# Seven gate panels ahead of the RWKV chunk solve, four between its small products, five left for later

## The chip, the cores and the metric

The kernel runs on one core of a Trainium2 chip. The metric is the device time in microseconds of one execution: 2214.5 us before the change, the median of three runs (2211.7 to 2218.17). One further execution was recorded by the hardware profiler; all rows below come from it.

## The reference

A block with four attention mixers and a feed-forward layer is followed by a second block, and only that one is touched. Its 512 tokens of width 1024 are projected once, and the projection is split into an RWKV-7 branch, a sparse-attention branch (DSA) and 2048 gate columns:

```
z = rmsnorm(h, norm_mix) @ w_in
z_rw, z_dsa, z_gate = _split(z, (RW_COLS, DSA_COLS, GATE_COLS))
y_a = rwkv7_branch(z_rw, ...)
y_b = dsa_branch(z_dsa, kv_norm, w_uk, w_uv)
g_a, g_b = jnp.split(jax.nn.sigmoid(z_gate + b_gate), 2, axis=-1)
h = h + (g_a * (y_a @ w_proj_a) + g_b * (y_b @ w_proj_b)) @ w_out
h = h + cross_attention(...); h = h + hier_moe(...)
# rwkv7_branch: a state of 64 x 64 for each of 8 heads, token by token
    sa = jnp.einsum('bhij,bhj->bhi', state, -kk_t)
    state = state * w_t + sa[..., None] * (kk_t * a_t) + v_t[..., None] * k_t
    y_t = jnp.einsum('bhij,bhj->bhi', state, r_t)
# dsa_branch: an indexer scores all keys for every query and keeps the best
    iscore = jnp.einsum('bqh,bqhs->bqs', w_idx, relu(q_idx . k_idx));  _, idx = lax.top_k(iscore, k_sel)
    softmax attention of 8 heads over the selected latent keys
```

The gates z_gate depend on nothing but the normed input, so they can be computed at any time before the two branches are merged.

## The kernel before

A gate panel is 128 of the 2048 gate columns. Its product is summed over eight blocks of 128 inputs, and each float32 weight and input is split into a high and a low fp32r part, so one panel is 24 matmuls of 128x512 (high by high, high by low, low by high; `mm3`, line 135). `panel` loads the raw weights in two halves by DMA on SyncE's (SP's) queue, casts the high part on ScalarE (ACT, line 125) and subtracts to get the low part on GpSimd (POOL, line 128). `fills` computes panels as fillers: they write PSUM buffers "f" of their own and use a pool of weight buffers that doesn't stand in the way of the work beside them. The result goes through a tanh on ACT and to DRAM (`gtd`).

The RWKV recurrence is computed in chunks of 64 tokens, 8 chunks for 4 pairs of heads:
- `rwkv_prep` makes the chunks' matrices (`Mt`) and values (`VA`).
- `rwkv_solve` solves the triangular system of each chunk. `from_values` (line 1365) makes products of 64x64 into `LV`, copied out of two PSUM buffers "s" by ACT and VectorE (DVE) in turn. The inverse of 128 triangular blocks of 32x32 is done on DVE alone (lines 1387 and 1389, 62 dependent operations); its input NT and its results Z go through DRAM. Then TensorE (PE) puts the halves together: 64 products of 32x32 (line 1409), 64 more (line 1417), and 128 products of 64x64 (lines 1423 and 1426).
- `rwkv_scan` carries the state over the eight chunks, `rwkv_out` normalizes by head (group norm) and applies the RWKV output gate.

`dsa_index` (lines 1533 to 1580) projects the indexer's queries and keys (into PSUM "tp"), scores (lines 1559 and 1560) and takes the best keys of three query blocks by 16 rounds each of MAX8 (line 1571) and MATCH_REPLACE (line 1572) on DVE. `dsa` attends; its first softmax operation is line 245. Behind it come the other gates as fillers and `mem_kv`, the keys and values of the memory for the cross attention.

What sets the order: a list scheduler gives each engine a fixed queue of instructions. It goes through the program in the order in which it is written and takes what its model of the readiness allows, earlier lines first, so a line that is written early is preferred and one that is written late fills gaps. `tc.issue_after` fixes an order between instructions beyond that. On the chip each engine takes its queue strictly in order. Before, the gates 0 to G2_AHEAD - 1 = 7 are written behind `dsa_index`, and the gates 8 to 15 behind `dsa`.

Of the kernel before, what the change touches and what calls it, by code (L numbers as in the profile page):

```python
# [20 lines left out]
G_BUFS = 18  # L21
G2_BUFS = 7
BD_BUFS = 2
G2_AHEAD = 8
DI_BUFS = 6
DG_BUFS = 10
DB_BUFS = 8
# [18 lines left out]
class Core:  # L46
# [90 lines left out]
    def fills(self, items, hi, lo, n=T, how=True):  # L137

        self.filling = how
        for src, done in items:  # L140
            done(self.fm(src, hi, lo, n))
        self.filling = False

    def acc(self, name="acc"):
        if name not in self.pb:
# [1205 lines left out]
        nc.sync.dma_start(kbd[:, :, p].rearrange("c p t -> p c t"), KB)  # L1351


def rwkv_solve(K, pool, Mt, VA, Wm):

    nc, tc, a = K.nc, K.tc, K.a
    nd = tc.dram_tile([P, 1024], F32, name="ndd")
    zd = tc.dram_tile([P, 2, 1024], F32, name="zdd")

    def from_values(i):  # L1360
        t = pool.tile([P, 2, 512], F32, name="LV", bufs=3)
        for s in range(2):
            pl = K.acc("s")
            for c in range(8):
                nc.tensor.matmul(pl[64:128, c * 64:(c + 1) * 64], Mt[0:64, i, s, c, 0:64],
                                 VA[0:64, i, c, 64 * s:64 * s + 64], start=True, stop=True, tile_position=(0, 64))
            K.copy(t[64:128, s], pl[64:128])
        return t

    LV = [from_values(i) for i in range(3)]  # L1370

    with nc.allow_non_contiguous_dma(reason="blocks"):
        for i in range(4):
            for b in range(2):
                nc.sync.dma_start(bass.AP(tensor=nd.tensor, offset=nd.offset + (i * 32 + b) * 1024,
                                          ap=[[32, 32], [2048, 16], [1, 32]]),
                                  Mt[64 + 32 * b:96 + 32 * b, i].rearrange("p s c t -> p (s c) t")[:, :, 32 * b:32 * b + 32])
    NT = pool.tile([P, 32, 32], F32, name="NT")
    nc.sync.dma_start(NT.rearrange("p a b -> p (a b)"), nd)
    Z = pool.tile([P, 32, 32], F32, name="Z")  # L1380
    nc.sync.dma_start(Z.rearrange("p a b -> p (a b)"),
                      bass.AP(tensor=a["eye32"].tensor, offset=a["eye32"].offset, ap=[[0, P], [1, 1024]]))
    for s in range(31):
        w = pool.tile([P, 256], F32, name="ztmp", bufs=1)
        n = 31 - s
        wv = w[:, :(s + 1) * n].rearrange("p (j t) -> p j t", t=n)
        nc.vector.tensor_mul(wv, Z[:, :s + 1, s:s + 1].to_broadcast([P, s + 1, n]),
                             NT[:, s:s + 1, s + 1:].to_broadcast([P, s + 1, n]))
        nc.vector.tensor_add(Z[:, :s + 1, s + 1:], Z[:, :s + 1, s + 1:], wv)
    nc.sync.dma_start(zd[:, 0], Z.rearrange("p a b -> p (a b)"))  # L1390
    nc.vector.tensor_copy(NT, Z.rearrange("p a b -> p b a"))
    nc.sync.dma_start(zd[:, 1], NT.rearrange("p a b -> p (a b)"))
    T1 = Wm.rearrange("p i c t -> p (i c t)").rearrange("p (i s c t) -> p i s c t", i=4, s=2, c=8)
    with nc.allow_non_contiguous_dma(reason="blocks"):

        nc.sync.dma_start(T1[64:96].rearrange("p i s c t -> p (i s c) t"),
                          bass.AP(tensor=zd.tensor, offset=zd.offset + 1024, ap=[[32, 32], [4096, 64], [1, 32]]))
        for b in range(2):
            nc.sync.dma_start(Mt[64 + 32 * b:96 + 32 * b].rearrange("p i s c t -> p (i s c) t")[:, :, 32 * b:32 * b + 32],
                              bass.AP(tensor=zd.tensor, offset=zd.offset + b * 2048,  # L1400
                                      ap=[[32, 32], [4096, 64], [1, 32]]))
    tags = ("acc", "pv", "s", "s")
    Q = Wm.rearrange("p i c t -> p i (c t)")
    for i in range(4):
        pq = K.acc(tags[i])
        for s in range(2):
            for c in range(8):
                o = (s * 8 + c) * 32
                nc.tensor.matmul(pq[96:128, o:o + 32], Mt[64:96, i, s, c, 32:64], T1[64:96, i, s, c], start=True,
                                 stop=True, tile_position=(64, 96))  # L1410
        K.copy(Q[96:128, i], pq[96:128])
    for i in range(4):
        pz = K.acc(tags[i])
        for s in range(2):
            for c in range(8):
                o = (s * 8 + c) * 32
                nc.tensor.matmul(pz[64:96, o:o + 32], Q[96:128, i, o:o + 32], Mt[96:128, i, s, c, 32:64], start=True,
                                 stop=True, tile_position=(96, 64))
        K.copy(Mt[64:96, i, :, :, 32:64], pz[64:96].rearrange("p (s c t) -> p s c t", s=2, c=8))
    for i in range(4):  # L1420

        pw, pu = K.acc(tags[i % 2]), [K.acc("s") for _ in range(2)]
        one = lambda s, c: nc.tensor.matmul(pw[64 * s:64 * s + 64, c * 64:(c + 1) * 64],
                                            VA[64:128, i, c, 64 * s:64 * s + 64], Mt[64:128, i, s, c, 0:64], start=True,
                                            stop=True, tile_position=(64, 64 * s))
        two = lambda s, c: nc.tensor.matmul(pu[s][64:128, c * 64:(c + 1) * 64], Mt[64:128, i, s, c, 0:64],
                                            LV[i][64:128, s, c * 64:(c + 1) * 64], start=True, stop=True,
                                            tile_position=(64, 64))
        for c in range(8):
            two(0, c)  # L1430
            one(0, c)
            two(1, c)
            one(1, c)
        K.copy(Wm[:, i].rearrange("p c t -> p (c t)"), pw)
        for s in range(2):
            K.copy(VA[64:128, i, :, 64 * s:64 * s + 64], pu[s][64:128].rearrange("p (c t) -> p c t", c=8))
        if i == 0:
            LV.append(from_values(3))
# [462 lines left out]
class Experts:  # L1901
# [305 lines left out]
def block2(K, h3, xd, out):  # L2207
# [20 lines left out]
    rwkv_prep(K, K.pool(S, "prep"), hhi, hlo, Mt, VA, eC, xg, kbd, red, bvd)  # L2228
    S.close()
    K.dve_split = ()  # L2230
    DS = ExitStack()
    dp = K.pool(DS, "dsa", "left")
    V = ExitStack()
    vp = K.pool(V, "solve")
    Wm = vp.tile([P, 4, 8, 64], F32, name="Wm")
    I_ = ExitStack()
    rwkv_solve(K, K.pool(I_, "inv"), Mt, VA, Wm)
    I_.close()
    rwkv_scan(K, K.pool(V, "scan"), Mt, VA, Wm, eC, kbd, red, ytd)
    V.close()  # L2240
# [4 lines left out]
    def gate(f):
        def done(z):
            t = rp.tile([P, 512], F32, name="gt", bufs=2)
            nc.scalar.activation(t, z, AF.Tanh, scale=0.5, bias=K.pd["bg"][:, f:f + 1])
            nc.sync.dma_start(gtd[f], t)
        return done  # L2250

    idx = dsa_index(K, dp, hhi, hlo)
    for f in range(G2_AHEAD):
        K.fills([(a["w2f"][22 + f], gate(f))], hhi, hlo, how=f%4==0 or 'main')
    DA = ExitStack()
    datt = K.pool(DA, "datt")
    mk = K.pool(DA, "memkv")
# [212 lines left out]
```

## Time and profile before

| | |
|---|---|
| median of 3 runs | 2214.5 us (2211.7 to 2218.17) |
| the profiled execution: its time, its span | 2219.63 us, 2217.7 us |
| mean granted clock of TensorE | 0.966 |
| busy: PE, DVE, ACT, POOL | 2061.6, 1082.7, 712.7, 486.9 us |
| the second block's stretch from rwkv_prep to the first softmax of dsa | about 1104 to 1342 us |

All times of rows are microseconds from the span's start. PE is the queue of matmuls; the granted clock is the share of full speed (2.4 GHz) that the chip allowed it, 1.00 or 0.50 at a time, a mean over a window. "Busy" on PE includes matmuls that run at half clock. A float32 product of 32x32 or 64x64 has two records, so x32 is 16 products.

### The profile page before, as it was taken

The numbers are of one execution on the slowest core, as the hardware profiler recorded it, in microseconds if no ns is written. First come the engines' busy times: TensorE is split into PE (matmuls) and PEld (weight loads), VectorE is DVE, ScalarE is ACT, GpSimd is POOL, SyncE is SP. The second block draws the span as 40 slices with busy tenths as digits, with TensorE's granted clock in tenths as the row PEclk, the third lists the DMA queues.
The fourth block names the chain that finished last, engine by engine and source line by source line (L and its number), as shares of the span: only waits on it lengthen the run. The fifth ranks groups of instructions, "written<-read, shape, count | busy, mean of one in ns | idle before, by whom it ended". The sixth has DMA issues, their size and how long they took to land. (4 is left out here: it accounts for less than half of the span.)

```text
span 2217.7 us, 28574 instructions
## 1 busy us (share of the span) xinstructions
PE 2061.6 (93%) x10308; PEld 1484.6 (67%) x10308; DVE 1082.7 (49%) x2569; ACT 712.7 (32%) x1510; POOL 486.9 (22%) x389
## 2 busy tenths in 40 slices
PE   6999899999999999978989999999998899998997
PEld 5767676686888888866777867777887344433333
DVE  5272326337763545465787646556444333332223
ACT  4353234423453434334432235543440111000012
POOL 2402232233233222233332121232121000000000
PEclk9999999999999999999998899999998899999999
DMA  5513332257232333133434342475256899999996
GB/s 175 174 44 84 75 104 80 72 175 233 84 118 95 95 97 102 52 113 112 119 109 101 105 163 89 145 252 188 70 188 217 335 419 420 420 420 420 419 421 248
DMA packets 175577, 407.50 MB, mean 184 GB/s; under 512 B 46922, under 2 KB 65482, under 8 KB 150728
## 3 DMA queue, kind: packets, MB, share of 16 engines
q1 hardware_dynamic: 173128, 400.07, 50.8%
q0 software_dynamic: 2304, 5.57, 0.7%
q8 instruction: 83, 1.36, 0.3%
q14 instruction: 62, 0.51, 0.1%
HBM read 370.94 MB, written 33.13 MB: 182 GB/s over the span
## 5 line engine op out<-in xcount | busy, mean ns | idle before, releaser
L128 POOL TENSOR_TENSOR w<-wraw,w 128x512 fp32r<-128x512 f32 x310 | 409.3, 1331 | 1068.1 <-ACT w L125 966.2
L125 ACT CAST w<-wraw 128x512 fp32r<-128x512 f32 (+1 forms) x446 | 261.8, 616 | 238.0 <-issue 51.9
L135 PE MATMUL f<-hhi,w 128*128 128x512 f32 (+1 forms) x832 | 279.7, 408 | 1.6 <-POOL w L128 0.6
L135 PE MATMUL f<-h2hi,w 128*128 128x512 f32 (+1 forms) x672 | 203.9, 384 | 0.4 <-POOL w L128 0.4
L128 DVE TENSOR_TENSOR w<-wraw,w 128x512 fp32r<-128x512 f32 (+1 forms) x136 | 112.5, 829 | 165.0 <-ACT w L125 160.7
L135 PEld LDWEIGHTS f<-hhi,w 128*128 128x128 f32 x832 | 160.5, 198 | 34.8 <-issue 3.2
L135 PE MATMUL acc<-hhi,w 128*128 128x512 f32 (+1 forms) x512 | 168.6, 396 | 11.1 <-DVE ks L1233 7.4
L135 PE MATMUL f<-hlo,w 128*128 128x512 f32 (+1 forms) x416 | 169.1, 407 | 0.2 <-DVE hlo L187 0.2
L135 PEld LDWEIGHTS f<-h2hi,w 128*128 128x128 f32 x672 | 125.3, 188 | 25.4 <-POOL w L128 0.6
L135 PE MATMUL f<-h2lo,w 128*128 128x512 f32 (+1 forms) x336 | 129.1, 384 | 0.0
L2096 PE MATMUL s<-mw,hT 128*64 128x512 f32 x416 | 107.0, 596 | 14.6 <-DMA mw<-wexp 14.6
L135 PEld LDWEIGHTS acc<-hhi,w 128*128 128x128 f32 x512 | 95.9, 190 | 35.0 <-DVE ks L1233 7.6
L2049 PE MATMUL f<-mw,xT 128*64 128x512 f32 x416 | 108.6, 597 | 10.8 <-DMA mw<-wexp 10.6
L135 PE MATMUL acc<-hlo,w 128*128 128x512 f32 (+1 forms) x256 | 100.7, 393 | 0.0
L135 PEld LDWEIGHTS f<-hlo,w 128*128 128x128 f32 x416 | 82.2, 198 | 16.0 <-issue 1.4
L2004 POOL DMA_INDIRECT xs<-xnd,row x13 | 12.9, 991 | 336.9 <-DVE tg L2009 282.6
L2096 PEld LDWEIGHTS s<-mw,hT 128*64 128x64 f32 x416 | 35.8, 137 | 74.5 <-issue 47.6
L2049 PEld LDWEIGHTS f<-mw,xT 128*64 128x64 f32 x416 | 33.2, 137 | 75.3 <-issue 50.2
L2100 DVE SCALAR_TENSOR_TENSOR ylo<-s,tg,yhi 128x512 fp32r<-128x512 f32 x32 | 24.0, 751 | 114.9 <-ACT yhi L2099 114.9
L2099 ACT ACTIVATE yhi<-s,tg 128x512 fp32r<-128x512 f32 x32 | 22.0, 687 | 168.9 <-PE s L2096 162.7
L135 PEld LDWEIGHTS f<-h2lo,w 128*128 128x128 f32 x336 | 63.2, 188 | 12.5
L135 PE MATMUL f<-w,mw 128*128 128x512 f32 x240 | 63.9, 413 | 2.1 <-ACT w L125 1.5
(762 smaller groups left out, 4070.5 us busy)
## 6 DMA issues: line engine op xcount, KB each, us to landing
mw<-wexp SPq DMA_DIRECT2D x155, 1024.0 KB
w<-wexp SPq DMA_DIRECT2D x36, 1024.0 KB
wraw<-wup SPq DMA_DIRECT2D x88, 256.0 KB
wraw<-w2f SPq DMA_DIRECT2D x76, 256.0 KB
wraw<-wgate SPq DMA_DIRECT2D x64, 256.0 KB
wraw<-wdown SPq DMA_DIRECT2D x44, 256.0 KB
wraw<-w1f SPq DMA_DIRECT2D x40, 256.0 KB
gated<-gt SPq DMA_DIRECT2D x28, 256.0 KB
```

The source lines that it names most:

```text
L125: nc.scalar.copy(hi[:, s], raw)
L128: eng.tensor_sub(lo[:, s], raw, hi[:, s].bitcast(F32))
L135: self.nc.tensor.matmul(out, l, r, start=start and i == 0, stop=stop and i == 2)
L2004: nc.gpsimd.indirect_dma_start(xs, None, self.xnd, bass.IndirectOffsetOnAxis(ap=row[:, 0:1], axis=0), bounds_check=T - 1, oob_is_err=False)
L2049: K.last = nc.tensor.matmul(GU[n][w][64 * s:64 * s + 64], xTs[n][:, kk, 64 * s:64 * s + 64], ws[s][k], start=kk == 0, stop=kk == 7)
L2096: K.last = nc.tensor.matmul(o[64 * s:64 * s + 64], hT[:, c, 64 * s:64 * s + 64], ws[s][c], start=c == 0, stop=c == 3)
L2099: nc.scalar.activation(yhi[:, hs], o, AF.Copy, scale=tgs[n][:, 1:2])
L2100: nc.vector.scalar_tensor_tensor(ylo[:, hs], o, tgs[n][:, 1:2], yhi[:, hs].bitcast(F32), op0=OP.mult, op1=OP.subtract)
```

## The change

The gates 0 to 6 (G2_PREP) are now written as fillers ahead of `rwkv_solve`. The gates 7 to 10 (up to G2_AHEAD, now 11) come from a generator, `steps`, three matmuls at a time (eight steps for a gate; the next panel's load is written one gate ahead). `rwkv_solve` calls it through `between`, which puts the small products and the steps into a fixed order: a step behind each sixteen products in the two 32x32 stages, and one or two in turn behind each eight products in the 64x64 stage, 32 steps in all. Five gates instead of eight stay behind `dsa`.

```
@@ -140 @@
+    def steps(self, items, hi, lo):
+        pans = []
+        for n, (src, done) in enumerate(items):
+            self.filling = True
+            pans += [self.panel(s, 1024) for s, _ in items[len(pans):n + 2]]
+            o = self.acc("f")
+            self.filling = False
+            for k in range(8):
+                s = slice(k * P, (k + 1) * P)
+                w = [t[:, s] for t in pans[n]]
+                for i, (a, b) in enumerate(((0, hi), (0, lo), (1, hi))):
+                    self.last = self.nc.tensor.matmul(o, w[a], b[:, k, :], start=k == 0 and i == 0, stop=k == 7 and i == 2)
+                if k == 7:
+                    done(o)
+                yield
@@ rwkv_solve @@
+    def between(products, n):
+        for i in range(0, len(products), n):
+            with tc.issue_after(K.last.ins) if K.last else nullcontext():
+                for p in products[i:i + n]:
+                    K.last = p()
+            with tc.issue_after(K.last.ins):
+                for _ in range(1 + count[0] % 2 if n == 8 else 1):
+                    next(fill, None)
+            count[0] += 1
...
-        for s in range(2):
-            for c in range(8):
-                o = (s * 8 + c) * 32
-                nc.tensor.matmul(pq[96:128, o:o + 32], Mt[64:96, i, s, c, 32:64], T1[64:96, i, s, c], start=True, ...
+        between([lambda s=s, c=c, o=o: nc.tensor.matmul(pq[96:128, o], ...) for s, c, o in at], 16)
...
-        for c in range(8):
-            two(0, c)
-            one(0, c)
-            two(1, c)
-            one(1, c)
+        between([lambda f=f, s=s, c=c: f(s, c) for c in range(8) for f, s in ((two, 0), (one, 0), (two, 1), (one, 1))], 8)
@@ block2 @@
-    rwkv_solve(K, K.pool(I_, "inv"), Mt, VA, Wm)
+    for f in range(G2_PREP):
+        K.fills([(a["w2f"][22 + f], gate(f))], hhi, hlo, how=f % 4 == 0 or "main")
+    fill = K.steps([(a["w2f"][22 + f], gate(f)) for f in range(G2_PREP, G2_AHEAD)], hhi, hlo)
+    rwkv_solve(K, K.pool(I_, "inv"), Mt, VA, Wm, fill)
...
     idx = dsa_index(K, dp, hhi, hlo)
-    for f in range(G2_AHEAD):
-        K.fills([(a["w2f"][22 + f], gate(f))], hhi, hlo, how=f%4==0 or 'main')
```

The line numbers of the changed program are higher: line 135 is 136 and 157 (in `steps`), 178 is 196, 1365 is 1396, 1387 and 1389 are 1418 and 1420, 1409 is 1438, 1423 and 1426 are 1451 and 1454, 1571 and 1572 are 1595 and 1596.

PE where the solve begins, before: the 32x32 products stand in one block between fillers (`f<-`, gate panels).

```order
L135 MATMUL f<-hhi,w 128x512 x2
L135 MATMUL f<-hlo,w 128x512
L135 MATMUL f<-hhi,w 128x512 x2
L135 MATMUL f<-hlo,w 128x512
L1409 MATMUL acc<-Wm,Mt 32x32 x16
L1409 MATMUL pv<-Wm,Mt 32x32 x16
L1409 MATMUL s<-Wm,Mt 32x32 x32
L135 MATMUL f<-hhi,w 128x512 x2
L135 MATMUL f<-hlo,w 128x512
L135 MATMUL f<-hhi,w 128x512 x2
L135 MATMUL f<-hlo,w 128x512
```

And after, from the same place, where index projections (`tp<-`) come first:

```order
L136 MATMUL tp<-hhi,w 128x512 x2
L136 MATMUL tp<-hlo,w 128x512
L1438 MATMUL acc<-Wm,Mt 32x32 x16
L157 MATMUL f<-hhi,w 128x512
L157 MATMUL f<-hlo,w 128x512
L157 MATMUL f<-hhi,w 128x512
L1438 MATMUL pv<-Wm,Mt 32x32 x16
L157 MATMUL f<-hhi,w 128x512
L157 MATMUL f<-hlo,w 128x512
L157 MATMUL f<-hhi,w 128x512
L1438 MATMUL s<-Wm,Mt 32x32 x16
L157 MATMUL f<-hhi,w 128x512
```

Each group of sixteen products has three gate matmuls behind it. In the 64x64 stage, before, 128 products stood without a wide matmul among them for most of the stage; after:

```order
L1454 MATMUL s<-LV,Mt 64x64 x2
L1451 MATMUL acc<-Mt,VA 64x64
L157 MATMUL f<-hhi,w 128x512
L157 MATMUL f<-hlo,w 128x512
L157 MATMUL f<-hhi,w 128x512
L1454 MATMUL s<-LV,Mt 64x64
L1451 MATMUL acc<-Mt,VA 64x64
L1454 MATMUL s<-LV,Mt 64x64
L1451 MATMUL acc<-Mt,VA 64x64
L1454 MATMUL s<-LV,Mt 64x64
L1451 MATMUL acc<-Mt,VA 64x64
```

Here a group is eight products. Ahead of the solve, PE after the change, at the end of 160 fillers in a row and the first values of `from_values`:

```order
L136 MATMUL f<-hhi,w 128x512 x2
L136 MATMUL f<-hlo,w 128x512
L136 MATMUL f<-hhi,w 128x512
L1396 MATMUL s<-VA,Mt 64x64 x16
L136 MATMUL tp<-hhi,w 128x512
L136 MATMUL tp<-hlo,w 128x512
L136 MATMUL tp<-hhi,w 128x512 x2
L1396 MATMUL s<-VA,Mt 64x64 x16
```

The second group (the second row of line 1396) writes the PSUM buffers that the copies of LV read. These copies on DVE, before, with the inversion's first operations behind them:

```order
L178 COPY KB<-tp 128x512
L178 COPY VA<-tp 128x512
L178 COPY LV<-s 64x512 x3
L1534 TENSOR_SCALAR widx<-tp 128x16
L1387 TENSOR_TENSOR ztmp<-Z,NT 128x31
L1389 TENSOR_TENSOR Z<-Z,ztmp 128x31
```

And after, with the inversion's last operations:

```order
L1418 TENSOR_TENSOR ztmp<-Z,NT 128x31
L1420 TENSOR_TENSOR Z<-Z,ztmp 128x31
L1422 COPY NT<-Z 128x1024
L196 COPY LV<-s 64x512 x3
L1558 TENSOR_SCALAR widx<-tp 128x16
L1573 TENSOR_TENSOR dg<-tp,qv 64x384 x2
L196 COPY Wm<-pv 32x512
```

The three copies went from ahead of the inversion to behind it. On DVE in `rwkv_out`, before, no round of the top-k is left:

```order
L187 TENSOR_TENSOR g<-YT,g 128x512
L1504 SCALAR_TENSOR_TENSOR YT<-acc,YT 128x512
L187 TENSOR_TENSOR g<-YT,g 128x512
L1504 SCALAR_TENSOR_TENSOR YT<-acc,YT 128x512
L227 TENSOR_TENSOR ss<-ss 128x1
L187 TENSOR_TENSOR g<-YT,g 128x512
L1504 SCALAR_TENSOR_TENSOR YT<-acc,YT 128x512
L187 TENSOR_TENSOR g<-YT,g 128x512
```

And after, at the same operations (lines 205 and 1528 are 187 and 1504 before):

```order
L205 TENSOR_TENSOR g<-YT,g 128x512
L1595 MAX m_10521<-mask_10450 128x8
L1528 SCALAR_TENSOR_TENSOR YT<-acc,YT 128x512
L1596 MATCH_REPLACE mask_10450<-m_10521,mask_10450 128x512
L1595 MAX m_10551<-mask_10525 128x8
L1597 TENSOR_SCALAR mask_10450<-mask_10450 128x512
L205 TENSOR_TENSOR g<-YT,g 128x512
L1596 MATCH_REPLACE mask_10525<-m_10551,mask_10525 128x384
L1528 SCALAR_TENSOR_TENSOR YT<-acc,YT 128x512
L1595 MAX m_10554<-mask_10525 128x8
```

A round (MAX, MATCH_REPLACE) stands ahead of nearly every operation. Of the 48 rounds, 8 stand in the scan now and 40 between it and the first operation of line 245; before, all 48 stood ahead of the operations shown.

## Rows read from the trace of the kernel before

**Rows 1.** The page: busy time, share and instructions of each engine.
```profile
PE 2061.6 (93%) x10308; PEld 1484.6 (67%) x10308; DVE 1082.7 (49%) x2569; ACT 712.7 (32%) x1510; POOL 486.9 (22%) x389
```

**Rows 2.** Windows over four stages around the solve; columns in the first row.
```profile
core 0: us, PE busy (x) PEld busy (x) DVE busy (x) ACT busy (x) POOL busy (x), PEclk, DMA share, GB/s
1106.00:1190.70 84.70, 73.96 (x363) 58.41 (x361) 72.73 (x156) 24.98 (x54) 27.20 (x20) 0.96 0.43 118
1190.70:1235.00 44.30, 44.30 (x579) 40.92 (x579) 18.29 (x40) 11.16 (x19) 6.21 (x7) 0.62 0.27 81
1235.00:1276.40 41.40, 39.35 (x268) 34.11 (x267) 31.30 (x85) 7.47 (x18) 4.83 (x4) 0.96 0.37 112
1276.40:1342.00 65.60, 61.01 (x250) 43.42 (x249) 31.84 (x86) 23.43 (x46) 16.93 (x13) 0.92 0.44 151
```

**Rows 3.** Windows inside the solve, the same columns.
```profile
1200.00:1205.00 5.00, 5.00 (x61) 3.99 (x61) 1.64 (x4) 0.29 (x1) 0.00 (x0) 0.89 0.69 204
...
1215.00:1235.00 20.00, 20.00 (x194) 18.73 (x193) 5.97 (x13) 6.13 (x11) 6.03 (x7) 0.50 0.23 73
```

**Rows 4.** Timeline of PE (start, us, line): a streak of fillers, ends.
```profile
1147.64 0.40 PE L135 MATMUL f<-hlo,w 128*128 128x512 f32 x1
...
1165.71 0.39 PE L135 MATMUL f<-hhi,w 128*128 128x512 f32 x1
```

**Rows 5.** Timeline of PE behind an idle.
```profile
1169.97 0.38 PE L1559 MATMUL tp<-dg,qv 128*128 128x256 f32 x1 [3.87 <-ACT big L1563]
...
1170.67 0.63 PE L135 MATMUL f<-hlo,w 128*128 128x512 f32 x1
...
1173.23 0.63 PE L135 MATMUL f<-hlo,w 128*128 128x512 f32 x1
```

**Rows 6.** Timeline of PE in the solve.
```profile
1190.74 1.19 PE L1409 MATMUL acc<-Wm,Mt 32*32 32x32 f32 x32
1191.77 1.17 PE L1409 MATMUL pv<-Wm,Mt 32*32 32x32 f32 x32
...
1207.64 0.58 PE L1423 MATMUL acc<-Mt,VA 64*64 64x64 f32 x9
...
1209.64 1.70 PE L1426 MATMUL s<-LV,Mt 64*64 64x64 f32 x14
...
1229.39 3.67 PE L1426 MATMUL s<-LV,Mt 64*64 64x64 f32 x32
...
1234.02 1.91 PE L1480 MATMUL pv<-Mt,VA 128*128 128x128 f32 x8
```

**Rows 7.** Timeline of DVE: the inversion, its first and last rows.
```profile
1119.35 1.06 DVE L1387 TENSOR_TENSOR ztmp<-Z,NT 128x31 f32<-128x31 f32 x1
...
1124.10 0.28 DVE L1389 TENSOR_TENSOR Z<-Z,ztmp 128x112 f32<-128x112 f32 x1
...
1125.79 0.34 DVE L1387 TENSOR_TENSOR ztmp<-Z,NT 128x175 f32<-128x175 f32 x1
1126.17 1.31 DVE L1389 TENSOR_TENSOR Z<-Z,ztmp 128x175 f32<-128x175 f32 x1
...
1170.09 1.08 DVE L1391 COPY NT<-Z 128x1024 f32<-128x1024 f32 x1
```

**Rows 8.** Timeline of POOL beside it.
```profile
1125.81 2.82 POOL L128 TENSOR_TENSOR w<-wraw,w 128x512 fp32r<-128x512 f32 x2 [2.96 <-ACT w L125]
```

**Rows 9.** Timeline of SP's queue: the load for the inversion.
```profile
1110.79 0.33 SPq L1379 DMA_DIRECT2D NT<-ndd  x1
```

**Rows 10.** Windows of lines 1571 and 1572 alone (DVE busy, count).
```profile
1100.00:1360.00 260.00, 26.51 (x48) 0.89 0.39 117
...
1100.00:1360.00 260.00, 29.52 (x96) 0.89 0.39 117
```

**Rows 11.** Timeline of DVE: the first softmax.
```profile
1341.94 0.29 DVE L245 CUSTOM_DVE_ANT_0 big<-s,dmask 128x128 f32<-128x128 f32 x1 [0.48 <-PE s L135]
```

More of the change, by code (lines that the diff above doesn't have):

```diff
@@ L23 @@
 BD_BUFS = 2
-G2_AHEAD = 8
+G2_PREP = 7
+G2_AHEAD = 11
 DI_BUFS = 6
@@ L1351, in rwkv_prep, with rwkv_solve @@
         nc.sync.dma_start(kbd[:, :, p].rearrange("c p t -> p c t"), KB)
-def rwkv_solve(K, pool, Mt, VA, Wm):
+def rwkv_solve(K, pool, Mt, VA, Wm, fill):
     nc, tc, a = K.nc, K.tc, K.a
+    count, K.last = [0], None
+    def between(products, n):
[7 more added lines that the diff above has]
+            count[0] += 1
     nd = tc.dram_tile([P, 1024], F32, name="ndd")
@@ L1403, in rwkv_solve @@
     Q = Wm.rearrange("p i c t -> p i (c t)")
+    at = [(s, c, slice((s * 8 + c) * 32, (s * 8 + c) * 32 + 32)) for s in range(2) for c in range(8)]
     for i in range(4):
         pq = K.acc(tags[i])
-        for s in range(2):
-            for c in range(8):
-                o = (s * 8 + c) * 32
-                nc.tensor.matmul(pq[96:128, o:o + 32], Mt[64:96, i, s, c, 32:64], T1[64:96, i, s, c], start=True,
-                                 stop=True, tile_position=(64, 96))
+        between([lambda s=s, c=c, o=o: nc.tensor.matmul(pq[96:128, o], Mt[64:96, i, s, c, 32:64], T1[64:96, i, s, c],
+                                                        start=True, stop=True, tile_position=(64, 96))
+                 for s, c, o in at], 16)
         K.copy(Q[96:128, i], pq[96:128])
@@ L1413, in rwkv_solve @@
         pz = K.acc(tags[i])
-        for s in range(2):
-            for c in range(8):
-                o = (s * 8 + c) * 32
-                nc.tensor.matmul(pz[64:96, o:o + 32], Q[96:128, i, o:o + 32], Mt[96:128, i, s, c, 32:64], start=True,
-                                 stop=True, tile_position=(96, 64))
+        between([lambda s=s, c=c, o=o: nc.tensor.matmul(pz[64:96, o], Q[96:128, i, o], Mt[96:128, i, s, c, 32:64],
+                                                        start=True, stop=True, tile_position=(96, 64))
+                 for s, c, o in at], 16)
         K.copy(Mt[64:96, i, :, :, 32:64], pz[64:96].rearrange("p (s c t) -> p s c t", s=2, c=8))
@@ L1428, in rwkv_solve @@
                                             tile_position=(64, 64))
-        for c in range(8):
-            two(0, c)
-            one(0, c)
-            two(1, c)
-            one(1, c)
+        between([lambda f=f, s=s, c=c: f(s, c) for c in range(8) for f, s in ((two, 0), (one, 0), (two, 1), (one, 1))], 8)
         K.copy(Wm[:, i].rearrange("p c t -> p (c t)"), pw)
@@ L2230, in block2, with gate, done @@
     K.dve_split = ()
+    def gate(f):
+        def done(z):
+            t = rp.tile([P, 512], F32, name="gt", bufs=2)
+            nc.scalar.activation(t, z, AF.Tanh, scale=0.5, bias=K.pd["bg"][:, f:f + 1])
+            nc.sync.dma_start(gtd[f], t)
+        return done
     DS = ExitStack()
@@ L2236, in block2 @@
     I_ = ExitStack()
-    rwkv_solve(K, K.pool(I_, "inv"), Mt, VA, Wm)
+    for f in range(G2_PREP):
+        K.fills([(a["w2f"][22 + f], gate(f))], hhi, hlo, how=f % 4 == 0 or "main")
+    fill = K.steps([(a["w2f"][22 + f], gate(f)) for f in range(G2_PREP, G2_AHEAD)], hhi, hlo)
+    rwkv_solve(K, K.pool(I_, "inv"), Mt, VA, Wm, fill)
+    for _ in fill:
+        pass
     I_.close()
@@ L2244, in block2 @@
     U.close()
[L2245 to L2250, printed above, removed]
     idx = dsa_index(K, dp, hhi, hlo)
-    for f in range(G2_AHEAD):
-        K.fills([(a["w2f"][22 + f], gate(f))], hhi, hlo, how=f%4==0 or 'main')
     DA = ExitStack()
```

## The prediction

> **What bounds the kernel now.** The page's busy times come first: TensorE is busy 2061.6 us of the span of 2217.7, 93% [rows 1], so only two things can win time, idle of PE and the clock at which it runs. The windows over the four stages between the end of rwkv_prep and the first softmax of dsa say where these lie [rows 2]. In 1106 to 1190.7, the stage before the solve, PE is idle 10.7 us (84.70 less 73.96) at a granted clock of 0.96. In the solve, 1190.7 to 1235, it is never idle (44.30 of 44.30), but the clock is 0.62: of its two levels, 2.4 and 1.2 GHz, it had the lower for most of the stage, and 0.38 x 44.3 = 16.8 us of full-speed work went. The scan to 1276.4 loses 2.1 us by idle, the stretch to 1342 another 4.6. So the solve's clock is the one large loss, and the windows inside it show what goes with it: 1215 to 1235, where PE is busy 20.00 of 20.00 almost only with the 64x64 products, was granted 0.50 throughout, and 1200 to 1205, mostly wide matmuls, had 0.89 [rows 3].
>
> The Trainium skill says in TensorE: Matmul & The Clock Gate, "Why this matters for your kernels", that drops inside a kernel are avoided by having no idle gaps between bursts. This trace doesn't agree for small products: no idle, and 0.50 [rows 3]. By that rule the interleaved matmuls would bring nothing here, since no gap is closed in the solve; it stands with rival 3.
>
> **The prices.** Wide matmul (128x512): 80 of them start between 1147.64 and 1165.71, 18.07/79 = 0.229 us each at full clock, and in all this streak PE never stood, so the panels' loads, casts and subtractions keep up with it [rows 4]. After an idle of 3.87 six of them took 1173.23 - 1170.67 = 2.56, 0.427 each: the half level [rows 5]. Sixteen 32x32 products (32 records) take 1.03 us, from start to start of two groups. Sixteen 64x64 products (32 records) take 2.00 us at full clock (1207.64 to 1209.64, 32 records) and 3.67 at half [rows 6].
>
> **Part one, seven gates ahead of the solve.** Gates 0 to 6 were fillers already; now they stand in front of the chunks' values. 160 of their 168 matmuls come as one streak from 1104.4: 160 x 0.229 = 36.6, to 1141.0. The first sixteen products of from_values (2.0) and four index matmuls (0.9) follow, to 1143.9. The next sixteen wait for a PSUM buffer that a VectorE copy of LV frees, and these copies now stand behind the whole inversion on DVE. Before, they stood ahead of it.
>
> So the inversion's end sets PE's restart. It has 62 dependent operations. Before, it ran from 1119.35, shared DVE with the index work, and ended before the copy of NT at 1170.09 [rows 7]. Alone, the row at 1124.10 gives 0.28 us for n = 112, and from this and its like I take 23.4 us for all 62 with the gaps. Beside a GpSimd subtraction (1125.81, two in 2.82 [rows 8]) an operation took 1.31, where its neighbour of the same size took 0.34 [rows 7]: 0.95 more, and two subtractions come per panel, every 24 x 0.229 = 5.5 us. Solving for the stretch, 23.4 + 1.9 x (length/5.5) gives 36; with a few that meet idle gaps I take 34 (bounds 23.4 and 36). Its start: NT's load was issued at 1110.79 [rows 9]; on SP's queue one more gate store now stands ahead of it, so I put it at 1112.8. The bounds are that moment and the old start of 1119.35; I take 1116.5. Then 34 + the copy of NT 1.1 + the copy of LV 0.7: PE may go on at 1152.3, a wait of 8.4 us (bounds 0 and 14).
>
> After it come 16 + 16 products (4.0), 4 + 16 + 35 index matmuls (12.6) and four transposes (0.5): 17.1. PE restarts at half clock; the six matmuls of rows 5 lost 6 x 0.198 = 1.2 us, and since small products come first here and this wait is twice as long, I take 3.5 (bounds 1.2 and the whole 17.1). The solve begins at 1173 (before: 1190.74). The inverse comes back in time: before, the first product stood 20.6 us behind the copy of NT and had other work ahead of it, and 1150.5 + 20.6 = 1171.
>
> **Part two, four gates between the solve's products.** 96 wide matmuls stand there now, against 29 fillers in a block before. At full clock: eight groups of sixteen 32x32 products and three wide matmuls, 8 x (1.03 + 0.8) = 14.6, where 0.8 is 3 x 0.229 and 0.1 for the change of shape; ten index matmuls 2.3; sixteen groups of eight 64x64 products, 16 x 1.0; behind them eight times three and eight times six wide matmuls, 8 x 0.8 + 8 x 1.47 = 18.2; from_values(3) 2.0. Sum 53.1, and one wait for a PSUM copy of 1 us: 54 us, to 1227 (before 1234, with 67 wide matmuls fewer, or 15.3 us of work). All of this rests on the clock staying up, bounded by "all at half": 96 x 0.198 + 288 x 0.052 = +34. I take full, because the window with wide matmuls among small ones was granted 0.89 [rows 3].
>
> **Part three, what makes room.** The index scores and the top-k move. PE had scored beside the inversion; now it does so in the scan, in the place of gate matmuls, and I leave the scan at its 42.4 us (1234.0 [rows 6] to 1276.4): it ends at 1269.4, 7 us earlier. But the top-k is 48 rounds on DVE, 26.51 + 29.52 = 56.0 us [rows 10], and was hidden beside the inversion, the solve and the scan. Now eight rounds run in the scan, and 40 between the scan's end and the first softmax: up to 40/48 x 56.0 = 46.7 us. DVE had 31.84 us of work in these 65.6 [rows 2]; 78.5 in all is more than the stretch. The rounds depend on each other, and rwkv_out's group norm now has a round ahead of each of its short operations; some 0.16 us between operations in 40 rounds make it 85 (bounds: 65.6, if all hides, and 97). The first softmax, 1341.94 before [rows 11], comes at 1269.4 + 85 = 1354.4, 12.5 us later.
>
> By then PE has done 42 wide matmuls more than it had before at this point (by the order of the instructions: 29 of gates, 13 of the latent queries), 42 x 0.229 = 9.6 us that need not be done later, and dsa and mem_kv behind it are bound by PE. Three gates fewer are left as fillers behind dsa; I cost that at nothing, because mem_kv's matmuls remain to fill its waits, and at up to 72 x 0.229 = 16.5 us if they don't. In the tail PE is idle some 21 us now (85 less the 61.01 of [rows 2] and 2.5 for eleven of the 42, which fall here), against 4.6, and the clock falls more often: 2 us. Sum: 12.5 - 9.6 + 2 = +4.9. The profiled execution took 2219.63 (its span and 1.9 around it), 5.1 above the median of 2214.5; the difference goes on the median: **2219.5**. What can be told from no change is about 0.3%, 6.6 us, so this is inside, on the slow side.
>
> **The rivals.** 1. The top-k hides. If the tail's DVE is not what ends last (PE has latent queries and gate fillers for it, and DVE's extra work needs an arrival only at each block's mask), the stretch keeps 65.6: 1269.4 + 65.6 - 1341.9 = -6.9, less 9.6, and 2 for the clock: -14.5, 2200. For it: DVE was 49% busy there. Against it: 78.5 us don't go into 65.6.
> 2. No wait at the LV copies: the inversion takes 23.4 and ends at 1141.7 with its copies, before PE comes. That saves 8.4 and a part of the restart: 2210. Against it are the GpSimd subtractions, seven panels' worth beside it.
> 3. The clock stays at half in the solve in spite of the wide matmuls; the streak before it then wins nothing and the 96 matmuls pay double: +34, 2253, slower. It decides from the moment PE's granted clock in the solve is under about 0.8. For it: six wide matmuls in a row were not enough at 1170.67 to raise it [rows 5], and here three or six stand together. Against it: the 0.89 of 1200 to 1205 [rows 3].
> 4. Nothing moves. These matmuls were fillers and are so now; what the solve wins the later stages lack, idle for idle: 2214.5.
> 5. The tail is worse than 85: each short operation of the group norm waits for a whole round, ScalarE and PE wait with it, and it takes 97: 2232.
>
> **How the numbers follow.** Forecast 0.42 (its own range 2211 to 2230: 0.01 faster, 0.19 the same, 0.22 slower); rival 1 0.22, all faster; rival 2 0.10 (0.03 faster, 0.07 the same); rival 3 0.08 and rival 5 0.08, slower; rival 4 0.10 (0.01, 0.08, 0.01). Faster 0.27, the same 0.34, slower 0.39. The range of 2200 to 2240 leaves out half of rival 1 and rival 3, 0.19.
>
> **What would show it.** Right: PE idle of some 8 us released by the DVE copy of LV, about 38 us behind rwkv_prep; granted clock above 0.9 in the solve; DVE nearly full from the scan's end to the first softmax, and that stretch some 20 us longer. Wrong: no idle before the second group of from_values (rival 2), a solve over 70 us (rival 3), a stretch from the scan to the first softmax of under 70 us (rival 1).

## The result

The changed kernel took 2239.89 us (median of four runs, 2236.11 to 2252.9), the kernel before 2213.68 us on the same chip (2211.7 to 2218.17). The ratio is 1.0122, 95% interval 1.0092 to 1.0153: slower by 26 us, clear of noise. The forecast was 2219.5 us and no measurable change, leaning to slower; the side was missed, and the time lies at the upper end of the range of 2200 to 2240.

The windows of the changed kernel over the same four stages, cut where they begin now (columns as in [rows 2]):

```profile
1106.00:1179.53 73.53, 65.54 (x338) 53.66 (x338) 38.76 (x75) 17.08 (x30) 21.24 (x17) 0.88 0.48 128
1179.53:1236.29 56.76, 56.76 (x651) 43.17 (x651) 7.61 (x11) 13.92 (x24) 13.46 (x12) 0.94 0.28 90
1236.29:1278.54 42.25, 40.60 (x286) 34.64 (x285) 35.80 (x77) 14.27 (x33) 5.08 (x4) 1.00 0.37 108
1278.54:1373.03 94.49, 72.90 (x273) 51.58 (x272) 74.99 (x213) 28.98 (x61) 19.39 (x15) 0.82 0.37 124
```

Against [rows 2]: the solve's clock rose from 0.62 to 0.94, which is what the change put the gates there for. The scan is as long as before (42.25 us). The stretch from the scan's end to the first softmax grew from 65.6 to 94.5 us. PE is idle there for 21.6 us (94.49 less 72.90; 4.6 before), and its clock is 0.82 (0.92 before). VectorE (DVE) is busy 75.0 us instead of 31.8.

PE's timeline at the places that the forecast names (it answers to [rows 5, 6]; line 252 is 234 before, the transposes of mem_norm):

```profile
1155.87 3.67 PE L1396 MATMUL s<-VA,Mt 64*64 64x64 f32 x32 [7.32 <-DVE LV L196]
...
1179.53 1.19 PE L1438 MATMUL acc<-Wm,Mt 32*32 32x32 f32 x32
1181.54 1.19 PE L1438 MATMUL pv<-Wm,Mt 32*32 32x32 f32 x32
...
1324.29 0.40 PE L136 MATMUL f<-hhi,w 128*128 128x512 f32 x1
1326.34 0.60 PE L1218 MATMUL acc<-ident,gn 128*16 128x128 f32 x4 [1.65 <-DVE gn L1215]
...
1366.46 1.94 PE L252 MATMUL tp<-ident,njunk 128*128 128x128 f32 x8 [9.44 <-DVE njunk L249]
```

The first row is the wait at the copies of LV, 7.32 us. The rows of 1179.53 and 1181.54 are two groups of sixteen products with three gate matmuls between them, 2.01 us. The row of 1324.29 is the last gate matmul ahead of the first softmax: behind it no gate is left to fill in, and PE idles step by step, in the last row 9.44 us for a DVE operation of mem_norm (line 249). Of the 21.6 us of idle 16.7 lie behind this matmul: from 1324.69 to 1373.03 PE is busy 31.68 of 48.34 us, at a clock of 0.75. On DVE that operation stands behind the rounds, and so does the first softmax (it answers to [rows 11]):

```profile
1360.54 0.41 DVE L1596 MATCH_REPLACE8 mask<-m,mask 128x256 f32<-128x256 f32 x1
1360.98 0.43 DVE L1595 MAX8 m<-mask 128x8 f32<-128x256 f32 x1
...
1365.57 1.41 DVE L249 SCALAR_TENSOR_TENSOR njunk<-njunk,ny,g_mem 128x512 f32<-128x512 f32 x2
...
1373.03 0.29 DVE L263 CUSTOM_DVE_ANT_0 big<-s,dmask 128x128 f32<-128x128 f32 x1 [0.44 <-PE s L136]
```

On DVE, ahead of the solve (answers to [rows 7]):

```profile
1120.95 0.97 DVE L1418 TENSOR_TENSOR ztmp<-Z,NT 128x31 f32<-128x31 f32 x1 [10.46 <-DMA NT<-ndd]
...
1126.33 1.31 DVE L1418 TENSOR_TENSOR ztmp<-Z,NT 128x175 f32<-128x175 f32 x1
1127.68 0.34 DVE L1420 TENSOR_TENSOR Z<-Z,ztmp 128x175 f32<-128x175 f32 x1
...
1154.06 1.03 DVE L1422 COPY NT<-Z 128x1024 f32<-128x1024 f32 x1
1155.12 0.69 DVE L196 COPY LV<-s 64x512 f32<-64x512 f32 x1
```

The inversion began at 1120.95 and lasted up to the copy of NT at 1154.06: 33.1 us, with 1.31 against 0.34 us for two operations of one size, one of them beside a GpSimd subtraction.

### The profile page after: what moved, and what is told of

The parts are those of the page before. It is cut to its first block, busy times and chain, and to the rows that moved or that the text cites. A ratio compares the mean times of both kernels' runs of the same rounds, so it can differ in the third digit from the quotient of the medians.

```text
span 2239.0 us, 28568 instructions
## 1 busy us (share of the span) xinstructions
PE 2069.9 (92%) x10308; PEld 1480.2 (66%) x10308; DVE 1075.0 (48%) x2569; ACT 714.1 (32%) x1510; POOL 483.3 (22%) x389
## 5 line engine op out<-in xcount | busy, mean ns | idle before, releaser
L136 PE MATMUL f<-hhi,w 128*128 128x512 f32 (+1 forms) x768 | 249.7, 398 | 1.9 <-ACT w L126 0.6
L136 PE MATMUL acc<-hhi,w 128*128 128x512 f32 (+1 forms) x512 | 173.3, 407 | 13.3 <-DVE ks L1251 7.5
L136 PEld LDWEIGHTS f<-hhi,w 128*128 128x128 f32 x768 | 144.3, 193 | 31.4 <-issue 2.5
L136 PE MATMUL f<-hlo,w 128*128 128x512 f32 (+1 forms) x384 | 152.4, 397 | 0.2 <-DVE hlo L205 0.2
L2073 PE MATMUL f<-mw,xT 128*64 128x512 f32 x416 | 108.6, 597 | 10.7 <-DMA mw<-wexp 10.5
L136 PEld LDWEIGHTS f<-hlo,w 128*128 128x128 f32 x384 | 74.1, 193 | 14.4 <-issue 1.0
L136 PEld LDWEIGHTS f<-h2lo,w 128*128 128x128 f32 x336 | 63.1, 188 | 12.3
```

Source lines behind the costliest of these rows:

```text
L136: self.nc.tensor.matmul(out, l, r, start=start and i == 0, stop=stop and i == 2)
L2073: K.last = nc.tensor.matmul(GU[n][w][64 * s:64 * s + 64], xTs[n][:, kk, 64 * s:64 * s + 64], ws[s][k], start=kk == 0, stop=kk == 7)
```

## The experiments

Theory A was that the top-k rounds displaced to DVE behind the scan are the loss by themselves; B, the wait at LV and the cold clock behind it; C, in this form after the first four runs, that the gates taken into the solve are missing as fillers behind the scan, where the rounds leave PE waiting; E, that interleaving costs by itself. Two of the first expectations use the letter C otherwise: for part one alone it is E, and for one round in the changed kernel it is the missing fillers without the rounds. Times are medians, each with its ratio to the kernel before on the same chip (median there 2209.4 to 2213.7 us). Single executions of one kernel differ by about 1%, so verdicts are drawn from ratios and the profile is read only for where time lies.

**Part one alone.** Built from the kernel before:

```
+    for f in range(7):
+        K.fills([(a["w2f"][22 + f], gate(f))], hhi, hlo, how=f % 4 == 0 or "main")
     rwkv_solve(K, K.pool(I_, "inv"), Mt, VA, Wm)
...
-    for f in range(G2_AHEAD):
+    for f in range(7, G2_AHEAD):
```

> The kernel before with the first part of the change alone: gates 0 to 6 written ahead of the solve, gate 7 behind dsa_index and gates 8 to 15 behind dsa as before; no gate matmul is put between the solve's products. By the order, 26 of the 48 top-k rounds now stand behind the scan (0 before, 33 in the changed kernel, counted from the first operation on YT). Theory A (the displaced top-k rounds on VectorE make the stretch from the scan's end to the first softmax long): the stretch takes about 80 us, the clock in the solve stays near 0.6, and the time is 2225 to 2240. Rival B (the wait for the LV copies behind the inversion and the cold clock after it is the main loss, the rest is neutral): 2213.7 + 7.3 + 4 = 2225, with a stretch of 66 us. Rival C (the interleaving is what costs, by the changes of shape in the solve): 2214.

Measured: 2212.79 us, ratio 0.9999 (0.9968 to 1.0031): no change. A and B missed the time, and the third theory (C there, E here) gave it with 2214. The stretch is near A's 80 us all the same; windows of the solve and of the stretch behind the scan:

```profile
1179.90:1215.84 35.94, 35.94 (x562) 34.19 (x561) 8.72 (x13) 9.17 (x17) 4.74 (x5) 0.67 0.21 66
...
1261.71:1351.16 89.45, 78.04 (x325) 56.56 (x325) 69.33 (x197) 31.58 (x60) 25.98 (x20) 0.94 0.45 148
```

The stretch is 89.45 us long and full of rounds (DVE 69.33), nearly as in the changed kernel. But PE is busy 78.04 us of it at a clock of 0.94: 183 filler matmuls (`f<-`) start in it, against 110 in the changed kernel's stretch and 121 in the kernel before. The long stretch behind the scan costs nothing here, where PE has work for it. The whole loss is thus in part two; whether by the changes of shape in the solve (E) or by the fillers that it takes from the stretch, this run doesn't tell.

**One round of the top-k instead of sixteen, in both kernels.**

```
-        for _ in range(16):
+        for _ in range(1):
             m8 = sm.tile([P, 8], F32, name="m8")
```

> The kernel before with one round of MAX8 and MATCH_REPLACE for each of the three query blocks instead of sixteen; 45 rounds of 48 are left out, and so the selected keys are others. This prices the top-k where it stands in the kernel before. Theory A: it was hidden beside the inversion, the solve and the scan, so the time stays within 7 us of 2213.7. Rival (the top-k always cost, in both kernels alike): 2190 to 2200, the same gain as in the changed kernel.

Measured: 2214.65 us, 1.0001 (0.9973 to 1.0029). The rounds cost the kernel before nothing.

> The changed kernel with one round for each of the three query blocks instead of sixteen, as in the run on the kernel before; 45 rounds of 48 are left out. Theory A: the stretch from the scan's end to the first softmax falls from 94.5 to about 66 us, and the time from 2239.9 to about 2212 (2205 to 2219). Rival B (LV wait and cold clock): the time stays at 2230 to 2240. Rival C (fewer fillers behind the scan): 2230 to 2240 too, with PE idle in the stretch unchanged.

Measured: 2225.02 us, 1.0020 (0.9989 to 1.0050). By the ratios 22 us of the 26 are gone; by the medians on this chip (2225.02 against 2211.42) only half, 13 us. The stretch:

```profile
1273.36:1349.68 76.32, 66.90 (x256) 45.80 (x256) 35.34 (x87) 25.47 (x55) 16.98 (x13) 0.87 0.39 136
```

It is 76.32 us instead of 94.49, and the solve is as in the changed kernel. So the rounds are a necessary part of half or more of the loss, and by the run with part one alone not a sufficient one. The expected 66 us was missed: with one round for each block PE is still idle 9.4 us there.

**The top-k ahead of the scan again.** `dsa_index` is called inside `rwkv_solve`, in the changed kernel:

```
+    idx = mid()
     tags = ("acc", "pv", "s", "s")
...
-    idx = dsa_index(K, dp, hhi, hlo)
```

> The changed kernel with one move: dsa_index is written inside rwkv_solve, behind the inversion and ahead of the 32x32 products, so the index scores and the top-k come ahead of the solve's copies in preference. By the order, no round stands behind the scan. All work is done. Theory A: the stretch from the scan's end to the first softmax goes back to 66 to 70 us and the time to 2205 to 2218, while the wait at the LV copies of about 7 us stays. Rival B: the time stays above 2230. Rival D (the rounds now stand in front of the solve's PSUM copies and stall PE there): the solve takes 75 us or more and the time stays above 2230.

Measured: 2229.07 us, 1.0082 (1.0052 to 1.0112): only a third of the loss gone.

```profile
1177.44:1246.31 68.87, 68.87 (x701) 51.62 (x701) 47.78 (x102) 26.02 (x55) 21.79 (x18) 0.95 0.31 104
1246.31:1299.37 53.06, 49.03 (x315) 40.92 (x314) 47.06 (x126) 12.88 (x28) 10.72 (x8) 1.00 0.35 109
1299.37:1357.85 58.48, 45.20 (x158) 31.30 (x158) 28.30 (x69) 16.45 (x33) 5.05 (x4) 0.71 0.39 133
```

No round stands behind the scan and the stretch is short, 58.48 us, but PE is idle 13.3 us of it at a clock of 0.71: the fillers are still missing. The solve (68.87) and the scan (53.06) took more, as rival D had it in direction; a part of that is index work that PE now does there (701 matmul records in the solve instead of 651, 315 in the scan instead of 286). The ranges of A and of D were both missed: the rounds are gone from the stretch, and most of the loss is still there.

**The four gates computed twice.** If PE lacks work behind the scan in the changed kernel, more work is free there:

```
     idx = dsa_index(K, dp, hhi, hlo)
+    for f in range(G2_PREP, G2_AHEAD):
+        K.fills([(a["w2f"][22 + f], gate(f))], hhi, hlo, how=f % 4 == 0 or "main")
```

> The changed kernel with 96 matmuls more: the gates 7 to 10, computed between the solve's products, are computed a second time as fillers written behind dsa_index. They give back to the stretch behind the scan the work that the change took out of it. Theory C, new (the stretch is as long as VectorE's work in it, and TensorE ran out of fillers there: the gates taken into the solve are missing, so it idles and falls to half clock): 96 x 0.229 = 22 us of work go mostly into the idle and the half clock; the time is 2238 to 2248, at most 8 above the changed kernel, and the granted clock in the stretch rises from 0.82 to over 0.92. Rival A (VectorE's rounds alone set the loss, fillers play no part, or TensorE is bound): the added work is paid in full, 2240 + 22 = 2262.

Measured: 2239.26 us, 1.0116 (1.0064 to 1.0169). 96 matmuls more, 22 us of work, and the time is that of the changed kernel.

```profile
1270.82:1362.86 92.04, 83.94 (x338) 62.09 (x337) 76.22 (x211) 32.02 (x67) 27.38 (x21) 0.91 0.43 145
```

PE is busy 83.94 us of a stretch of the same length (72.90 in the changed kernel), its clock 0.91 instead of 0.82 (expected: over 0.92). Over the whole execution PE's idle, the span less its busy time, is 155.0 us (2238.1 less 2083.1); it is 169.1 in the changed kernel (2239.0 less 2069.9) and 156.1 in the kernel before [rows 1]. The stretch itself hardly got shorter (92.04 us): more fillers don't shorten it, they use it.

The control, the same on the kernel before (gates 7 to 10 twice, behind `dsa_index`):

> The control of the run with gates computed twice: the kernel before, with the gates 7 to 10 computed a second time as fillers written behind dsa_index, 96 matmuls more. Theory C (the changed kernel had room for them, because TensorE ran out of fillers behind the scan, and the kernel before has none): 96 x 0.229 = 22 us, paid mostly, 2226 to 2236. Rival (fillers of this kind are nearly free in either kernel, so that they were free in the changed kernel says nothing): 2211 to 2219.

Measured: 2238.31 us, 1.0123 (1.0093 to 1.0154), 27 us more, a little above the expectation. There the work is paid in full. The kernel before with 96 matmuls too many (1.0123), the changed kernel (1.0122), and the changed kernel with 96 too many (1.0116) take the same time: the changed kernel leaves about as much PE time unused behind the scan as the gates between the products are worth.

**Two gates instead of four.** `G2_AHEAD = 9`.

> The changed kernel with two gates (7 and 8) instead of four between the solve's products: they last through the 32x32 stages and a part of the 64x64 stage; seven gates are left for behind the solve. Part one alone is the same as before (ratio 0.9999), all four gates cost 26 us. Theory C (gates between the products are missing as fillers behind the scan): the loss is less than half, since only a part of the idle is left: 2214 to 2226. Rival E (the interleaving itself costs, product by product and step by step): half of the steps, half of the loss, and the length of the stretch behind the scan doesn't differ from the changed kernel's 94.5 by over 3 us: 2225 to 2230.

Measured: 2229.91 us, 1.0068 (1.0042 to 1.0094), 15 us. Half of the gates, a little over half of the loss. The median lies at the end of E's range, and the ratio's 2226 us on this chip (1.0068 x 2211.07) at the edge of both ranges, so the time doesn't tell C from E. The profiled execution took 2251.03 us, the slowest of the ten; its stretch of 103.1 us is not within E's 3 us of the changed kernel's, but an execution that slow decides nothing.

**The copies of LV on ScalarE**, in the changed kernel and with part one alone.

```
-            K.copy(t[64:128, s], pl[64:128])
+            nc.scalar.copy(t[64:128, s], pl[64:128])
```

> The changed kernel with the six copies of LV ahead of the inversion all on ScalarE instead of ScalarE and VectorE in turn. TensorE then doesn't wait for the end of the inversion. Expected by the term of the prediction (the wait of 7.3 us and the half clock behind it): the solve begins 8 to 12 us earlier, at about 1169, and since all that follows hangs on it, the time falls to 2228 to 2233. Rival (the inverse comes back at the same time, so the solve's first product waits instead): the solve begins no more than 3 us earlier and the time stays within 3 us of the changed kernel.

Measured: 2232.40 us, 1.0102 (1.0073 to 1.0132). The median lies in the expected range, but it comes from another chip than the changed kernel's; by the ratios the gain is some 4 us instead of 7 to 12, and the two intervals overlap. The profile has the wait gone, the solve 12 us earlier, as expected, and at full clock:

```profile
1106.00:1167.47 61.47, 57.50 (x305) 46.27 (x303) 33.58 (x66) 17.76 (x31) 20.30 (x15) 0.94 0.49 134
1167.47:1221.19 53.72, 53.72 (x651) 40.99 (x651) 6.91 (x10) 14.40 (x25) 13.47 (x12) 1.00 0.28 95
...
1263.76:1355.17 91.41, 71.22 (x272) 50.01 (x272) 75.97 (x213) 28.88 (x61) 19.44 (x15) 0.85 0.38 128
```

The solve took 53.72 us, against the 54 of the forecast; the stretch behind the scan is idle for 20.2 us, as before.

> The kernel before with part one alone (gates 0 to 6 ahead of the solve, no gate between its products) and the six copies of LV on ScalarE. Part one alone measured the same as before. If the wait at LV is a loss of its own there, the time is 2199 to 2206; if the stretch behind the scan takes it up again (its length is VectorE's, which starts from the same index scores), it stays at 2209 to 2216.

Measured: 2215.28 us, 1.0019 (0.9990 to 1.0048): nothing won. B costs nothing by itself in this kernel.

**A version meant to beat both**: part one, LV on ScalarE, `dsa_index` inside `rwkv_solve`, no fixed order.

> A version meant to beat both: the kernel before with gates 0 to 6 ahead of the solve, no gate between its products by a fixed order, the copies of LV on ScalarE, and dsa_index written inside rwkv_solve behind the inversion, so that no round of the top-k stands behind the scan and nine gates are left as fillers. Theory C: the wait of 7 us at LV is gone, the stretch behind the scan is 60 to 66 us again and full of fillers: 2198 to 2208. Rival (the scores and rounds stand in front of the solve's copies, and TensorE waits in the solve or the scan for VectorE, as much as it wins): 2209 to 2220.

Measured: 2212.78 us, 0.9996 (0.9974 to 1.0017). The rival was right: the stretch is short (58.27) and the scan long:

```profile
1230.53:1299.95 69.42, 64.79 (x399) 51.49 (x398) 62.46 (x165) 17.78 (x38) 15.51 (x12) 1.00 0.36 114
1299.95:1358.22 58.27, 51.32 (x208) 37.23 (x207) 33.28 (x86) 19.50 (x39) 11.97 (x9) 0.85 0.46 160
```

**The whole pattern four gates earlier**, `G2_PREP = 3`, `G2_AHEAD = 7`, and the same with LV on ScalarE.

> The changed kernel with the whole pattern four gates earlier: gates 0 to 2 ahead of the solve, 3 to 6 between its products, nine left (G2_PREP 3, G2_AHEAD 7). By the order, the index work now fills the wait ahead of the solve, no round of the top-k stands behind the scan, and the stretch there has four gates more. All 96 matmuls still stand between the products. Theory C (the loss comes from fillers missing behind the scan while VectorE's rounds stretch it): the loss goes nearly whole, 2208 to 2222, and the clock in the solve stays above 0.9. Rival E (the interleaving itself costs): 2230 to 2245, as in the changed kernel.

Measured: 2231.37 us, 1.0086 (1.0050 to 1.0121). C's range failed, and so did its clock above 0.9; E's range holds the time:

```profile
1106.00:1181.30 75.30, 59.07 (x290) 45.39 (x288) 50.54 (x105) 20.66 (x39) 17.55 (x14) 0.82 0.45 123
1181.30:1247.74 66.44, 66.44 (x644) 50.04 (x644) 34.64 (x75) 14.05 (x31) 11.93 (x11) 0.74 0.17 59
...
1289.22:1355.64 66.42, 63.22 (x255) 43.83 (x254) 33.35 (x86) 23.88 (x46) 17.04 (x13) 0.90 0.43 149
```

Behind the scan all is as in the kernel before: 66.42 us, PE idle for 3.2. Ahead of the solve PE is now idle for 16.2 us (10.7 before [rows 2]), where the four gates are missing instead. But over the whole execution its idle is 154.3 us (2225.9 less 2071.6), no more than the 156.1 of the kernel before; what grew is its busy time, by 10.0 us, so missing fillers don't explain this loss. The solve takes 66.44 us at a clock of 0.74, with the same 96 gate matmuls between its products. It has 80 wide matmuls more than the solve of the run with part one alone and takes 30.5 us more, 12.2 above their price at full clock (80 x 0.229 = 18.3). Here the interleaving does cost, as E has it, and it does so where the clock is down. Windows of 5 us around the solve's start, of PE alone (busy, clock, DMA share, GB/s):

```profile
1176.00:1181.00 5.00, 4.20 (x19) 1.00 0.08 31
1181.00:1186.00 5.00, 4.93 (x69) 0.66 0.31 105
```

And inside it, with all columns, first of this run and then of the changed kernel:

```profile
1186.00:1191.00 5.00, 5.00 (x43) 3.44 (x44) 2.00 (x4) 0.58 (x1) 0.00 (x0) 0.50 0.01 3
1206.00:1211.00 5.00, 5.00 (x41) 3.85 (x38) 3.81 (x9) 2.23 (x4) 1.14 (x1) 0.50 0.15 54
1211.00:1216.00 5.00, 5.00 (x26) 3.32 (x26) 1.16 (x2) 0.00 (x0) 1.38 (x2) 0.50 0.30 105
1216.00:1221.00 5.00, 5.00 (x51) 3.91 (x52) 2.08 (x4) 1.17 (x2) 0.00 (x0) 0.93 0.02 3
```

```profile
1184.00:1189.00 5.00, 5.00 (x62) 3.95 (x60) 0.70 (x1) 0.58 (x1) 0.00 (x0) 0.59 0.02 5
1189.00:1194.00 5.00, 5.00 (x45) 3.89 (x43) 0.00 (x0) 0.00 (x0) 0.00 (x0) 0.73 0.00 0
1194.00:1199.00 5.00, 5.00 (x77) 3.69 (x76) 0.69 (x1) 1.43 (x3) 0.00 (x0) 1.00 0.01 3
1199.00:1204.00 5.00, 5.00 (x72) 3.96 (x73) 0.69 (x1) 3.10 (x6) 2.96 (x3) 1.00 0.32 105
```

Both kernels came into the solve at full clock, this one behind an idle of 0.88 us at 1180.2. Its clock fell within 2 us of the solve's start (0.50 from 1183 on) and stayed at half through the 32x32 stages and a part of the next, over 30 us, although three wide matmuls stood behind every sixteen products. In the changed kernel (1.00 from 1169 on) the clock fell in the first stage too, with PE busy 5.00 of 5.00, but it came back within a run of ten index matmuls (1189.38 to 1192.87), which this run's solve doesn't have.

> The same with the six copies of LV on ScalarE. By the order the index scores then fall into the scan again, and 26 rounds stand behind it, as in the run with part one alone, with some 170 fillers in the stretch. The candidate to beat both kernels: the wait at LV is gone, the clock in the solve is up, and the fillers are there. Theory C: TensorE is filled in the stretch, 2200 to 2214. Rival F (the long stretch behind the scan costs by itself, since PE still waits for each DVE operation in it): 2220 to 2235.

Measured: 2232.38 us, 1.0087 (1.0055 to 1.0120). Rival F gave the number, but not for its reason: this solve began at half clock, behind idles of 4.17 and 2.18 us, and kept it; its timeline of PE there:

```profile
1164.40 0.77 PE L1583 MATMUL tp<-dg,qv 128*128 128x512 f32 x1 [4.17 <-DMA qv<-dg]
...
1167.78 1.91 PE L1438 MATMUL acc<-Wm,Mt 32*32 32x32 f32 x32 [2.18 <-DMA Wm<-zdd]
1169.61 0.80 PE L157 MATMUL f<-hhi,w 128*128 128x512 f32 x1
```

Its windows of the solve and of the stretch behind the scan:

```profile
1167.78:1234.33 66.55, 66.55 (x641) 50.29 (x641) 6.92 (x10) 12.23 (x21) 8.46 (x8) 0.73 0.19 57
...
1278.76:1364.02 85.26, 75.03 (x318) 54.52 (x318) 70.14 (x196) 30.40 (x57) 25.36 (x19) 0.96 0.42 145
```

The stretch behind the scan was well filled (idle 10.2 us at 0.96). Over the whole execution PE's busy time is 11.3 us longer than in the kernel before (2072.9) and its idle 4.7 us (160.8): here too the larger part of the loss is busy time, with a solve as long as in the run before.

## Why the prediction was wrong

The order of things was as forecast: the wait at LV, the solve at a high clock, the top-k behind the scan, a late first softmax, and a part given back later. The first softmax came at 1373.03 instead of 1354.4, 18.6 us later than forecast, from four terms.

- The solve's start: forecast 1173, measured 1179.53, +6.5. The inversion began at 1120.95 instead of 1116.5, and took 33.1 us for the 34 of the forecast. PE's wait was 7.32 for 8.4. From its end to the solve 23.7 us went (1155.87 to 1179.53) for 20.6: PE ran 12.0 us at half clock, which costs 6.0 instead of the 3.5 put down, and idled 0.7.
- The solve's length: 54 forecast, 56.8 measured at a clock of 0.94; where the clock was 1.00, it took 53.7. The term is right in sum and partly by luck. At full clock (LV on ScalarE) the 32x32 stages took 16.0 us for 14.6, since a change of shape there and back costs 0.3 and not 0.1, and the 64x64 stage 35.3 for 37.2: its price, sixteen products in 2.00 us at full clock, was read in rows at which the clock was 0.58 (1207.6 to 1209.7). The one dip in the first stage was not foreseen. Nor did the 0.89 of [rows 3] bear the full clock that was taken: its wide matmuls stand in one block, and 1195 to 1200, all wide, was granted 0.50. Rival 3, the clock that stays low, did not come in this kernel, but did in two of the experiments.
- The scan: 42.4 forecast, 42.3 measured.
- **The stretch behind the scan**, the step that failed: 85 forecast, 94.5 measured, +9.5. VectorE's work in it was sized well, 75.0 us for 78.5. Mis-sized were its waits: the forecast put 0.16 us between operations in 40 rounds, 6.5 us, and VectorE stood idle 19.5 us (94.49 less 74.99), 10.3 of them waiting for ScalarE and 8.0 for PE. That is the mechanism of rival 5 (97 us, 2232), which had a chance of 0.08. PE's idle was forecast well, 21 us for 21.6. The 2 us put down for its clock were too few: of its busy time in the stretch 24.7 us ran at half clock, 12.3 us at the worth of full speed, against 5.1 before, 7.2 more. But the clock is not what sets the length: with the gates computed twice it was 0.91, and the stretch still took 92.0 us.
- What is given back: 31.1 us late at the first softmax, 21.3 at the end of the span (2239.0 less 2217.7). The 9.8 between them is the credit of 9.6 for 42 matmuls.

Behind the wrong size stands a wrong account. The forecast charged the long stretch to the displaced top-k alone and credited the interleaving with the solve's clock. The runs show that both parts are needed for the loss. Part one alone puts 35 of the 48 rounds behind the scan (39 in the changed kernel, by the trace) and costs nothing (0.9999), because the gates that are left fill the stretch. Part two takes those four gates away. What it wins is nothing: in the run of part one alone the solve took 35.94 us at a clock of 0.67 with 16 wide matmuls in it (13 of the index projections, 3 of the scores), in the changed kernel 56.76 with ten and the 96 of the gates. 90 more for 20.8 us is 0.231 each, their ordinary price of 0.229 at full clock: the higher clock paid for the changes of shape and no more. So the changed kernel's loss is not in its solve, as theory E would have it; in the two runs with the whole pattern four gates earlier, where the solve fell to half clock, the larger part of it is. And the 16.8 us that the forecast read from the clock in [rows 2] were never to be had. With LV on ScalarE the interleaved solve had the clock at 1.00 throughout and took 53.72 us; less 90 x 0.229 = 20.6 that is 33.1 for the rest, against 35.94 in the run of part one alone: 2.8 us, where 0.33 x 35.94 = 11.9 stand in the clock. A part of the difference goes to the switches: sixteen 32x32 products take 2.01 - 3 x 0.229 = 1.32 us between wide matmuls, 1.03 in a row.

What stays open: the split of the 26 us. In the two profiled executions 13.0 of the 21.3 us are idle of PE (156.1 to 169.1) and 8.3 longer busy time, but single executions differ by as much as these terms. Open is also why the clock held in one interleaved solve and fell in two; and whether a version with the gates where they were, a solve that keeps its clock and the copies of LV off the inversion's way would beat the kernel before. None of the versions that were run did.

## What to carry to other kernels

Fillers are a stock: before moving them, look for the stage that lives on them now, and test it by adding work there; if extra work is free, the stage is starved. A low granted clock over small matmuls isn't its distance from 1.00 in time: price the stage by its own rows at both levels, with the switches of shape. And a stretch bound by another engine cost nothing here as long as the busiest engine had other work to do in it.

## What the runs showed of the hardware

The same pattern of sixteen 32x32 products and three 128x512 matmuls went three ways. It held the full clock in the changed kernel with LV on ScalarE (1.00 throughout). It lost it with PE never idle in the changed kernel (0.59 in 1184 to 1189), where the clock came back within a run of ten 128x512 matmuls, and with the pattern four gates earlier (1.00 in 1176 to 1181, 0.50 from 1183 on). And it did not raise the clock from half in over 30 us, in that run and in the same with LV on ScalarE, whose solve began at half clock; sixteen products, up to the next wide matmul, took 1.83 us in the latter (1167.78 to 1169.61) instead of 1.12 in the changed kernel (1179.53 to 1180.65). In both runs the clock rose only behind the first six wide matmuls that stand together, in the 64x64 stage. What decides between holding and losing the clock is not shown.

The Trainium skill (TensorE: Matmul & The Clock Gate, "Why this matters for your kernels") wants bursts without idle gaps between them. The cold start behind the idles of 4.17 and 2.18 us agrees with it; half clock that lasts for 30 us with no idle doesn't.
